# A hybrid decoder layer: down weights in 8 KB rows, other regions split, and some work ahead

## The chip, the core and the metric

The kernel runs on one core of a Trainium2 chip. The metric is the device time of one execution in microseconds. Engines are named as the profile names them: PE (matmul), PEld (weight load of PE), DVE (vector), ACT (scalar), POOL (GpSimd) and SP, whose queue issues nearly all the large loads. "Clock" is the TensorE clock that the throttle granted, as a share of full speed (1.0 is 2.4 GHz, 0.5 is 1.2 GHz).

## What is computed

One layer over 256 tokens of width 1024, in float32. What fills most of the time is the mixture of experts: 4 groups of 8 experts; every token goes to the best group and to two experts in it. The kernel streams the weights of all 32 experts (6 MB each) from memory.

```python
h = h + concat(pool_mixer(z), fox_attention(z)) @ w_out     # z = rms_norm(h) @ w_in
t = rms_norm(h)                                             # 256 x 1024
for g in range(4):                                          # top-1 group, top-2 experts in it
    hg = einsum('nd,edf->nef', t, w_e_gate[g])              # 8 x 1024 x 512
    hu = einsum('nd,edf->nef', t, w_e_up[g])                # 8 x 1024 x 512
    a  = silu(hg) * hu * comb[:, g, :, None]
    y  = y + einsum('nef,efd->nd', a, w_e_down[g])          # 8 x 512 x 1024
h = h + y
h = h + sigmoid(rms_norm(h) @ w_ple_gate) * (p @ w_ple_proj)
out = rms_norm(h)
```

## The kernel before

**Stages.** The first 105 us are the mixer (input projection, pooling, attention, output projection) and the start of the routing. Then tokens are sorted into slots by one-hot matrices: each expert has 32 slots, four experts (a quad) fill 128. `count` counts the tokens ahead of each, `first_slots` and `first_gather` make the one-hots of the first quad and gather its tokens, transposed, into `xg`. Experts then run as 16 pairs `pi` of experts 2pi and 2pi+1; pairs 2q and 2q+1 are quad `q`, quads 2g and 2g+1 are group `g`. Last stands the pair 15, which is written out by hand.

**A pair.** `gate_up(pi, 0)` and `gate_up(pi, 1)` multiply the gathered tokens by gate and up weights (rows k 0 to 3 and 4 to 7 of the 8 that lie in each partition, "kh0" and "kh1"); `hidden` applies SiLU; `hidden_transposes` turns the hidden activations; `down` multiplies by the down weights; `stack` evicts. `fill(pi, 0..3)` stands between these and runs small work planned for that place (`plan(pair, fill 0, fill 1, fill 2, fill 3)`): the gather of the next quad (`gather`, L910), its scatter weights (`scatter_weights`: DVE makes `oc`, L919, PE transposes it into `sw`, L922), the scatter of a finished quad (L982), and for a finished group the gate of the embedding: `turn` transposes its rows (L1097, evicted by DVE into `fin`, L1098), `z_direct` multiplies them by the gate weights `wpg` (L1108), `finish` writes the group's rows out. The order of instructions on PE, DVE and ACT is the written one (a manual schedule).

**The stream.** `load_pair(pi)` issues the twelve 1 MB loads of a pair on SP's queue (gate, up, then down), one pair ahead of their users. They go into 20 regions of 1 MB in SBUF (128 partitions of 8 KB), which `queue` hands out in turn; a region is free for its next load when the last reader of its old content is done. Three of the regions are pairs of half-regions, ("8a","8b"), ("9a","9b") and ("5a","5b"); a load into such a pair is two loads of 0.5 MB (`stream`, L798), a load into a whole region one (L801). Seven entries leave the ring: `xrows` (rows of a group), `PP` (embedding projections), `r_ht` (the turned rows `fin`) and four of gate weights `wpg`, so that 13 MB remain. Eight loads can be under way; the ninth issue waits until the eighth before it has landed.

**Rows.** Gate and up weights are laid out `(p k) f`: in a whole region a partition takes 4 rows of 512 floats that lie side by side in memory, 8 KB. Down weights are `(c p) d`: a partition takes two rows of 1024 floats that lie apart, 4 KB each. A load into half a region has rows of 4 KB too.

**The quarters.** Beside the regions lie four 4 KB-wide buffers Q0 to Q3 (`quarter`) in which `xg`, `ys`, attention tiles and others take turns.

Of the kernel before, what the change touches and what calls it, by code (L numbers as in the profile page):

```python
# [25 lines left out]
def layer_kernel(ctx, tc, x, p, g_mix, w_in, b_f, w_pool, s_pool, w_out, g_ffn, w_grp, b_grp,  # L26
# [575 lines left out]
    def half_logits(tb, dh):  # L602
        if dh == 0:
            psls[tb] = acc(f"ps_l{tb}")
        for k in range(4):
            nc.tensor.matmul(psls[tb][:, 0:36], lhsT=tTs[tb][:, dh, k, :], rhs=wr[:, dh, k, :],
                             start=dh == 0 and k == 0, stop=dh == 1 and k == 3)
# [90 lines left out]
    square_half(1, 1)  # L698
    half_transposes(1, 1)
    count(0)  # L700
    half_logits(1, 0)
# [85 lines left out]
    wd_v = w_e_down[0].rearrange("g e (c p) d -> (g e) p c d", p=128)  # L787
# [16 lines left out]
    def whole_region():  # L804
        return queue.pop(next(n for n, i in enumerate(queue) if not isinstance(i, tuple)))
# [9 lines left out]
    def load_last():  # L815

        gu, dn, used = {}, {}, []
        for j in range(2):
# [5 lines left out]
            for h in range(2):  # L824
                part = wd_v[e, :, :, 512 * h:512 * h + 512] if j else wd_v[e, :, 2 * h:2 * h + 2, :]
                dn[j, h] = stream(f"wd{e}{h}", part)[1]
# [3 lines left out]
    def load_pair(pi):  # L830
# [26 lines left out]
    Xc, auxc, rowi, smalls = {}, {}, {}, {}  # L857
# [13 lines left out]
    def compact(g):  # L871
# [7 lines left out]
        Xc[g] = xrows[:, (g % 2) * 1024:(g % 2 + 1) * 1024]  # L879
# [24 lines left out]
    def gather(q, kh, orr):  # L904
# [3 lines left out]
        pg = tb_(f"pgx{q}{kh}")  # L908
# [6 lines left out]
    def scatter_weights(q, oq):  # L915

        oc = wk.tile([128, 128], F32, tag="c2", name=f"oc{q}")
        e = 3 + 4 * (q % 2)
        nc.vector.tensor_tensor(oc.rearrange("p (e s) -> p e s", e=4), oq.rearrange("p (e s) -> p e s", e=4),  # L919
                                auxc[q // 2][:, e:e + 4, None].to_broadcast([128, 4, 32]), op=ALU.mult)  # L920
        pw = tb_(f"sw{q}p")
        nc.tensor.transpose(pw[:, 0:128], oc, ident)  # L922
# [70 lines left out]
    def embedding(p_in, wpp):  # L993
        psp = tb_("ps_p")
        for k in range(2):
            for tb in range(2):
                nc.tensor.transpose(psp[:, k * 256 + tb * 128:k * 256 + (tb + 1) * 128],
                                    p_in[:, tb, k * 128:(k + 1) * 128], ident)
        pT = wk.tile([128, 2, T], F32, tag="a", bufs=3, name="pT")
        nc.vector.tensor_copy(pT, psp.rearrange("p (k t) -> p k t", k=2))  # L1000
        for i in range(4):
# [4 lines left out]
            nc.scalar.copy(PP[:, i // 2, (i % 2) * 512:(i % 2 + 1) * 512], ps)  # L1006
# [25 lines left out]
    yss = {0: quarter(1, "ys0")}  # L1032
# [4 lines left out]
    xrows = region(whole_region(), "xrows")  # L1037
    compact(0)
    oq, orr = one_hots(0)
    scatter_weights(0, oq)  # L1040
    oq, orr = one_hots(1)
    stack(1, pd, yss[0])
    for kh in range(2):
        gather(1, kh, orr)
    scatter_weights(1, oq)
# [41 lines left out]
    def fin_tile(g):  # L1087

        return (big.tile([128, 2048], F32, tag="X", name=f"fin{g}") if g == LG else region(r_ht, f"fin{g}"))
# [3 lines left out]
    def turn(g, mh):  # L1093
        hT = fins[g][:, 0:1024].rearrange("p (m t) -> p m t", m=8)
# [66 lines left out]
    def dense_path():  # L1161
        tD = region(r_ht, "tD").rearrange("p (k t) -> p k t", k=8)
        for tb in range(2):
            for kh in range(2):
# [3 lines left out]
                nc.vector.tensor_copy(tD[:, 4 * kh:4 * kh + 4, tb * 128:(tb + 1) * 128],  # L1168
# [8 lines left out]
        for k in range(8):  # L1177
            nc.vector.scalar_tensor_tensor(tD[:, k, :], tD[:, k, :], gf[:, k:k + 1], rbd,
# [384 lines left out]
```

## Time and profile before

| | |
|---|---|
| median of 3 runs | 594.89 us (594.45 to 595.76) |
| the profiled execution | 595.37 us |
| its span (first to last instruction) | 593.8 us |
| mean granted clock | 0.929 |
| PE busy, share of the span | 89% |
| DVE, ACT, POOL busy | 29%, 20%, 7% |
| bytes read from memory | 220.93 MB |

The profiled execution is 0.48 us over the median of the runs, and 1.6 us of it lie around the span.

### The profile page before, as it was taken

The page shows a single profiled execution, that of the slowest core. Times are in us where ns is not written, and L with a number is a line of the kernel's source. Part 1 is how long each engine was busy: PE and PEld are TensorE (multiplying, and loading weights), DVE is VectorE, ACT ScalarE, POOL GpSimd, SP SyncE. Part 2 cuts the span into 40 slices and gives each one's busy share as a digit, 9 for nine tenths or more (in the row PEclk, how much of TensorE's full clock was granted, in tenths as well). Part 3 has the DMA queues.
Part 4 walks back from the last instruction along what each step waited for, and adds up shares of the span by engine and source line. Part 5 has one row for each costly group of instructions (what it writes and reads, how often), then busy time and mean ns, then how long its engine had stood idle before and what let it go on. Part 6 is the DMA issues. An engine that isn't in the chain of part 4 may idle for free.

```text
span 593.8 us, 7947 instructions
## 1 busy us (share of the span) xinstructions
PE 527.2 (89%) x3201; PEld 258.7 (44%) x3201; DVE 174.1 (29%) x453; ACT 116.2 (20%) x245; POOL 40.6 (7%) x83
## 2 busy tenths in 40 slices
PE   8999999888879997898789589989989889999991
PEld 7889778632423442232224143324343343334450
DVE  5768765422211122000141112042111120125124
ACT  4544553300101002000121001031101010102123
POOL 6087000000000000000000000000000000000100
PEclk9999999798889897899888799999998979999996
DMA  8989966599999999999999999999999999999920
GB/s 284 345 289 414 389 259 247 216 390 418 408 416 412 423 409 421 419 416 419 413 421 413 419 408 421 410 418 412 417 411 416 413 415 412 417 412 415 412 107 17
DMA packets 55734, 222.54 MB, mean 375 GB/s; under 512 B 8714, under 2 KB 15630, under 8 KB 42254
## 3 DMA queue, kind: packets, MB, share of 16 engines
q1 hardware_dynamic: 55086, 220.94, 93.3%
q0 software_dynamic: 608, 1.05, 0.5%
q8 instruction: 26, 0.43, 0.3%
q14 instruction: 14, 0.11, 0.0%
HBM read 220.93 MB, written 2.10 MB: 376 GB/s over the span
## 4 chain that ended last, share of the span: by engine, by line
PE 47%; DMA 38%; issue 6%; DVE 4%; ACT 2%; SPq 1%; POOLq 0%; POOL 0%; DVEq 0%; ACTq 0%
DMA wu<-in_w_e_up_dram 23%; PE pg L936 11%; DMA wd<-in_w_e_down_dram 9%; PE pd L964 5%; PE po L277 4%; PE Z L1108 3%; PE zl L1270 3%; DMA wpg<-in_w_ple_gate_dram 3%; PE pgx L910 2%; DMA wg<-in_w_e_gate_dram 2%; PE ps_k L277 2%; PE ps_q L277 1%; PE g L663 1%; PE pp L1004 1%; PE xc L884 1%
## 5 line engine op out<-in xcount | busy, mean ns | idle before, releaser
L936 PE MATMUL pg<-wu,xg 128*32 128x512 f32 x480 | 129.1, 639 | 13.8 <-DMA wu<-in_w_e_up_dram 13.8
L936 PE MATMUL pg<-wg,xg 128*32 128x512 f32 x472 | 122.3, 640 | 7.4 <-PEq L1393 5.2
L964 PE MATMUL pd<-wd,at 128*32 128x512 f32 x480 | 69.7, 710 | 3.1 <-issue 1.5
L1108 PE MATMUL Z<-wpg,fin 128*128 128x512 f32 x128 | 59.5, 606 | 2.1 <-DVE fin L1098 2.1
L943 DVE TENSOR_TENSOR act<-act,pg 64x512 f32<-64x512 f32 x15 | 10.4, 692 | 168.9 <-ACT act L942 168.9
L936 PEld LDWEIGHTS pg<-wg,xg 128*32 128x32 f32 x472 | 27.0, 116 | 63.1 <-issue 52.7
L936 PEld LDWEIGHTS pg<-wu,xg 128*32 128x32 f32 x480 | 30.8, 116 | 48.9 <-DMA wu<-in_w_e_up_dram 27.4
L942 ACT ACTIVATE act<-pg 64x512 f32<-64x512 f32 x15 | 8.8, 588 | 177.9 <-PE pg L936 177.9
L964 PEld LDWEIGHTS pd<-wd,at 128*32 128x32 f32 x480 | 16.8, 127 | 48.7 <-issue 44.6
L1108 PEld LDWEIGHTS Z<-wpg,fin 128*128 128x128 f32 x128 | 22.9, 189 | 34.5 <-issue 31.7
L972 DVE COPY ys<-pd 64x512 f32<-64x512 f32 x15 | 10.4, 694 | 85.5 <-ACT ys L971 78.8
L910 PE MATMUL pgx<-oq,xrows 128*128 128x128 f32 x112 | 30.6, 427 | 2.9 <-DVE xg L912 2.4
L1157 POOL DMA_INDIRECT out_dram<-fin,rowi x3 | 3.0, 1003 | 424.3 <-DVE ing L868 281.8
L910 PEld LDWEIGHTS pgx<-oq,xrows 128*128 128x128 f32 x112 | 27.6, 332 | 9.3 <-issue 4.2
L971 ACT COPY ys<-pd 64x512 f32<-64x512 f32 x15 | 8.6, 577 | 78.5 <-PE pd L964 78.5
L1270 PE MATMUL zl<-wpg,yT 128*64 128x512 f32 x96 | 23.2, 605 | 0.0
L277 PE MATMUL po<-sp_o,cTh 128*128 128x512 f32 x64 | 20.8, 405 | 0.0
L1131 PE MATMUL ppc<-PP,ing 128*128 128x512 f32 x32 | 14.8, 601 | 2.0 <-DVE ing L868 1.7
L912 DVE TENSOR_TENSOR xg<-pgx,gf 128x512 f32<-128x512 f32 x14 | 9.7, 692 | 18.6 <-PE pgx L910 18.6
L884 PE MATMUL xc<-X,ing 128*128 128x512 f32 x32 | 14.7, 602 | 0.0
L982 PE MATMUL Y<-ys,sw 128*128 128x512 f32 x28 | 13.9, 618 | 0.7 <-ACTq L1393 0.7
L277 PE MATMUL ps_k<-aTh,sp_k 128*128 128x256 f32 x64 | 12.6, 290 | 0.0
(361 smaller groups left out, 683.8 us busy)
## 6 DMA issues: line engine op xcount, KB each, us to landing
wu<-in_w_e_up_dram SPq DMA_DIRECT2D x52, 1024.0 KB, 16.3
wg<-in_w_e_gate_dram SPq DMA_DIRECT2D x49, 1024.0 KB, 16.8
wd<-in_w_e_down_dram SPq DMA_DIRECT2D x49, 1024.0 KB, 17.7
wd<-in_w_e_down_dram SPq DMA_DIRECT2D x30, 512.0 KB, 15.0
wg<-in_w_e_gate_dram SPq DMA_DIRECT2D x28, 512.0 KB, 15.2
wu<-in_w_e_up_dram SPq DMA_DIRECT2D x24, 512.0 KB, 15.2
w_o<-in_w_out_dram SPq DMA_DIRECT2D x4, 1024.0 KB, 5.7
wpg<-in_w_ple_gate_dram SPq DMA_DIRECT2D x4, 1024.0 KB, 15.7
```

The lines of the kernel that those rows point to most:

```text
L277: nc.tensor.matmul(o, lhsT=a, rhs=b, start=first and i == 0, stop=last and i == 2)
L884: nc.tensor.matmul(px, lhsT=pg_[:, tb, :], rhs=X[:, tb, ds], start=tb == 0, stop=tb == 1)
L910: nc.tensor.matmul(pg[:, k4 * 128:(k4 + 1) * 128], lhsT=Xc[q // 2][:, 4 * kh + k4::8], rhs=orr, start=True, stop=True)
L912: nc.vector.tensor_tensor(xgs[q][:, 4 * kh:4 * kh + 4, :], pg.rearrange("p (k t) -> p k t", k=4), gf[:, 4 * kh:4 * kh + 4, None].to_broadc ...
L936: nc.tensor.matmul(pg[32 * c:32 * c + 32, :], lhsT=xg[:, k, sl:sl + 32], rhs=gu["gu"[c // 2], j, kh](k % 4), start=k == 0, stop=k == 7, ti ...
L943: nc.vector.tensor_mul(act[64:128, :], act[64:128, :], pg[64:128, :])
L964: nc.tensor.matmul(pd[32 * gI:32 * gI + 32, :], lhsT=at[:, c, 32 * j:32 * j + 32], rhs=dn[j, c // 2](c % 2)[:, dh * 512:(dh + 1) * 512], s ...
L972: nc.vector.tensor_copy(ys[rs, 512:1024], pd[64:128, :])
L982: nc.tensor.matmul(Ys[g][dh], lhsT=sws[q], rhs=ys[:, dh * 512:(dh + 1) * 512], start=q % 2 == 0, stop=q % 2 == 1 or last)
L1108: nc.tensor.matmul(Z[g][i], lhsT=hTs[g][:, m, :], rhs=wpg[m // 2](m % 2)[:, 512 * i:512 * i + 512], start=m == 0, stop=m == 7)
L1131: nc.tensor.matmul(pp, lhsT=ings[g][:, tb, :], rhs=PP[:, tb, ds], start=tb == 0, stop=tb == 1)
L1270: nc.tensor.matmul(zls[pi][64 * dh:64 * dh + 64, :], lhsT=yTs[pi][:, m, :], rhs=wpg[m // 2](m % 2)[:, dh * 512:(dh + 1) * 512], start=m == ...
```

## The change

Down weights are laid out `(f p c) d`: of each half `f` of the 512 hidden rows, a partition takes two rows that lie side by side in memory, 8 KB. The hidden index of partition p is then 256 f + 2 p + c, so `hidden_transposes` picks every second column. `wpp` (the embedding projection's weights) is laid out in the same way. `xrows`, `PP` and `r_ht` take the three pairs of half-regions out of the ring; before they took the whole regions 15, 0 and 12.

Half a load more goes out early: of the first down weights of expert 3, which wait for region 8a (and 9a) until the first pair's `gate_up` has read it, one half is loaded into the quarter Q1 (`wd_extra`), and `ys0`, which lay there, lies in Q3.

Work is written in another order at several places: `count(1)` ahead of the last two of the first gather; three of the logits of tokens 128 to 255 ahead of the transposes before them; `oc` (`spread_weights`, DVE) is made in fill 0, and the transpose `sw` stands ahead of both halves of the gather, whose second half goes to another PSUM bank; `turn` stands in fill 2 (ahead of `down`) and not in fill 3 in pairs 4, 8 and 12; `finish(2)` stands in fill 0 of pair 14; one of four `z_scatter` of the last pair stands ahead of `down1(1, 0)`.

```diff
     square_half(1, 1)
+    half_logits(1, 0, range(3))
     half_transposes(1, 1)
     count(0)
-    half_logits(1, 0)
+    half_logits(1, 0, (3,))
     half_logits(1, 1)
 ...
-    first_gather(0, range(6))
+    first_gather(0, range(4))
     choose_group(1)
     choose_experts(1)
     count(1)
+    first_gather(0, (4, 5))
 ...
-    wd_v = w_e_down[0].rearrange("g e (c p) d -> (g e) p c d", p=128)
+    wd_v = w_e_down[0].rearrange("g e (f p c) d -> (g e) p f c d", f=2, c=2)
 ...
-    def whole_region():
-        return queue.pop(next(n for n, i in enumerate(queue) if not isinstance(i, tuple)))
+    def two_halves(i, name):
+        return [big.tile([128, 1024], F32, tag=f"R{z}", name=f"{name}{n}") for n, z in enumerate(i)]
+    def split_region():
+        return queue.pop(next(n for n, i in enumerate(queue) if isinstance(i, tuple)))
 ...
-                i, dn[j, ch] = stream(f"wd{e}{ch}", wd_v[e, :, 2 * ch:2 * ch + 2, :])
+                if (e, ch) == (3, 0):
+                    extra = quarter(1, "wd_extra")
+                    nc.sync.dma_start(extra, wd_v[e, :, 0, 0, :])
+                    i = queue.pop(0)
+                    rest = big.tile([128, 1024], F32, tag=f"R{i[0]}", name="wd_rest")
+                    nc.sync.dma_start(rest, wd_v[e, :, 0, 1, :])
+                    dn[j, ch] = lambda r: rest if r else extra
+                else:
+                    i, dn[j, ch] = stream(f"wd{e}{ch}", wd_v[e, :, ch])
                 used.append(i)
 ...
+            f0 = 256 * (c // 2)
-            nc.tensor.transpose(pa[:, c * 64:(c + 1) * 64], act[64:128, c * 128:(c + 1) * 128],
+            nc.tensor.transpose(pa[:, c * 64:(c + 1) * 64], act[64:128, f0 + c % 2:f0 + 256:2],
                                 ident[64:128, 64:128])
 ...
-        i, wpp = stream("wpp", w_ple_proj[0].rearrange("(k p) c -> p k c", p=128))
+        i, wpp = stream("wpp", w_ple_proj[0].rearrange("(p k) c -> p k c", k=2))
 ...
-    yss = {0: quarter(1, "ys0")}
+    yss = {0: quarter(3, "ys0")}
 ...
-    xrows = region(whole_region(), "xrows")
+    xrows = two_halves(split_region(), "xrows")
 ...
     def new_quad(q):
         oqs[q] = one_hots(q)
+        spread_weights(q, oqs[q][0])
 ...
-        return ([lambda: gather(q, 0, oqs[q][1])], [lambda: gather(q, 1, oqs[q][1]),
-                                                    lambda: scatter_weights(q, oqs[q][0])])
+        return ([lambda: scatter_weights(q), lambda: gather(q, 0, oqs[q][1])],
+                [lambda: gather(q, 1, oqs[q][1], acc)])
 ...
-            plan(at, [], [], [], [lambda e=e: e < LG - 1 and new_fin(e), lambda e=e: turn(e, 0), lambda e=e: turn(e, 1),
-                                 lambda e=e: half_norm(e)])
+            plan(at, [], [], [lambda e=e: e < LG - 1 and new_fin(e), lambda e=e: turn(e, 0), lambda e=e: turn(e, 1)],
+                 [lambda e=e: half_norm(e)])
 ...
-            plan(at + 2, [], [], end[1:])
+            plan(at + 2, end[1:])
 ...
-            PP = region(whole_region(), "PP").rearrange("p (b d) -> p b d", b=2)
+            PP = two_halves(split_region(), "PP")
 ...
-            r_ht = whole_region()
+            r_ht = split_region()
 ...
     hidden_transposes1(1)
+    z_scatter(Q, range(2, 3), 96)
     down1(1, 0, dn[1, 0])
-    z_scatter(Q, range(2, 4), 96)
+    z_scatter(Q, range(3, 4), 96)
```

Of each wide buffer's two halves the code now takes `PP[tb]`, `fins[g][0]`, `fins[g][1]` and `xrows[g % 2]` where it took slices; the down weights of the last expert are cut into four loads of 0.5 MB, each of rows of 2 KB as before (two loads before).

Three places in the order of instructions show what moved. The first is SP's queue at the start of pair 3's loads, where `wg` and `wu` are gate and up weights and the shape's last numbers are the rows of floats in each partition. Before:

```order
L801 DMA wpp<-in_w_ple_proj_dram 128x2x1024
L801 DMA wg_1647<-in_w_e_gate_dram 128x2048
L798 DMA wg_1649<-in_w_e_gate_dram 128x1024
L798 DMA wg_1650<-in_w_e_gate_dram 128x1024
L798 DMA wu_1653<-in_w_e_up_dram 128x1024
L798 DMA wu_1654<-in_w_e_up_dram 128x1024
L798 DMA wu_1657<-in_w_e_up_dram 128x1024
L798 DMA wu_1658<-in_w_e_up_dram 128x1024
L801 DMA wg_1661<-in_w_e_gate_dram 128x2048
```

The same place with the change:

```order
L804 DMA wpp<-in_w_ple_proj_dram 128x2048
L804 DMA wg_1649<-in_w_e_gate_dram 128x2048
L804 DMA wg_1651<-in_w_e_gate_dram 128x2048
L804 DMA wu_1653<-in_w_e_up_dram 128x2048
L801 DMA wu_1655<-in_w_e_up_dram 128x1024
L801 DMA wu_1656<-in_w_e_up_dram 128x1024
L804 DMA wg_1659<-in_w_e_gate_dram 128x2048
```

Two of three split loads have become whole ones of 8 KB rows; behind this piece one down load is split, and none else but the last expert's.

The second is PE in pair 12, from the end of `gate_up` (`pg`) to the first rows of `down` (`pd`); `pgx` is the gather, `pa` the hidden transposes, `ht` the turned rows. Before:

```order
L936 MATMUL pg_3371<-wu_3226,xg_3279 32x512
L910 MATMUL pgx_3416<-oq_3390,xrows 128x128 x4
L949 MATMUL pa_3422<-ident,act_3412 128x64 x4
L910 MATMUL pgx_3429<-oq_3390,xrows 128x128 x4
L922 MATMUL sw7p<-ident,oc_3435 128x128
L964 MATMUL pd_3441<-wd_3228,at_3427 32x512
L964 MATMUL pd_3441<-wd_3230,at_3427 32x512
```

The same place with the change:

```order
L960 MATMUL pg_3322<-wu_3183,xg_3242 32x512
L946 MATMUL sw7p<-ident,oc_3344 128x128
L931 MATMUL pgx_3373<-oq_3341,xrows_1578 128x128 x4
L974 MATMUL pa_3379<-ident,act_3365 128x64 x4
L931 MATMUL pgx_3386<-oq_3341,xrows_1578 128x128 x4
L1127 MATMUL ht_3392<-ident,xrows_1577 128x128 x4
L1127 MATMUL ht_3398<-ident,xrows_1577 128x128 x4
L989 MATMUL pd_3404<-wd_3185,at_3384 32x512
```

The transpose `sw7p` has gone ahead of both gathers, and the turned rows have come in from behind the sixteen rows of `pd`.

The third is PE in the first routing; `g` is a gather of the first quad by the one-hot `or`, `ps_cs` the count. Before:

```order
L663 MATMUL g_1274<-or_1148,X 128x128
L663 MATMUL g_1276<-or_1148,X 128x128
L638 LDWEIGHTS triu_bf
L638 MATMUL ps_cs_1286<-oh,triu_bf 128x32
L638 LDWEIGHTS triu_bf
L638 MATMUL ps_cs_1286<-oh,triu_bf 128x32
L638 LDWEIGHTS ones_bf
L638 MATMUL ps_cs_1286<-oh,ones_bf 128x32
```

The same place with the change:

```order
L638 LDWEIGHTS triu_bf
L638 MATMUL ps_cs_1282<-oh,triu_bf 128x32
L638 LDWEIGHTS triu_bf
L638 MATMUL ps_cs_1282<-oh,triu_bf 128x32
L638 LDWEIGHTS ones_bf
L638 MATMUL ps_cs_1282<-oh,ones_bf 128x32
L638 LDWEIGHTS ones_bf
L638 MATMUL ps_cs_1282<-oh,ones_bf 128x32
L663 MATMUL g_1287<-or_1148,X 128x128
L663 MATMUL g_1289<-or_1148,X 128x128
```

The count has gone ahead of the last two gathers.

## Rows read from the trace of the kernel before

**Rows 1.** Windows: stretch, length; PE, PEld, DVE, ACT, POOL busy (count); clock; DMA share; GB/s.

```profile
120.00:468.00 348.00, 303.35 (x1570) 115.82 (x1562) 65.99 (x175) 39.77 (x79) 2.04 (x2) 0.91 1.02 415
482.00:563.00 81.00, 79.40 (x557) 30.91 (x553) 19.07 (x43) 10.37 (x23) 3.32 (x9) 1.00 1.02 414
```

**Rows 2.** Waits of PE, 230 to 470 us: waiter, waited for, total us, times, longest.

```profile
PE pg L936 <- DMA wu<-in_w_e_up_dram: 13.8, 11, 1.7
```

**Rows 3.** Timeline of PE, where its last wait for a load ends.

```profile
468.42 0.62 PE L936 MATMUL pg<-wu,xg 128*32 128x512 f32 x1 [1.47 <-DMA wu<-in_w_e_up_dram]
```

**Rows 4.** Waits of PE, 468 us to the end.

```profile
PE sw7p L922 <- DVE oc L919: 1.1, 1, 1.1
PE Z L1108 <- DVE fin L1098: 1.0, 1, 1.0
...
PE pd L1449 <- issue: 0.4, 1, 0.4
PE yt L1260 <- ACT ys L971: 0.4, 1, 0.4
PE pgx L910 <- DVE xg L912: 0.4, 1, 0.4
```

**Rows 5.** Expert 31's last gate load, 549.3 us: issue, time to landing; its first user.

```profile
L801 SPq DMA_DIRECT2D wg<-in_w_e_gate_dram x1: 328/328/328, 549.3 to 549.3; - x1
...
DMA to landing us min/median/max: 13.9/13.9/13.9
...
566.74 0.12 PEld L1427 LDWEIGHTS pg<-wg,xg 128*32 128x32 f32 x2
```

**Rows 6.** Windows of 8 us within the stream.

```profile
212.00:220.00 8.00, 8.00 (x55) 3.03 (x46) 1.84 (x3) 0.59 (x1) 0.00 (x0) 1.00 1.03 410
364.00:372.00 8.00, 8.00 (x43) 2.65 (x41) 0.93 (x6) 0.00 (x0) 0.00 (x0) 1.00 1.01 420
226.00:234.00 8.00, 6.97 (x42) 2.53 (x35) 2.26 (x6) 1.81 (x5) 0.00 (x0) 0.80 1.02 420
```

**Rows 7.** DMA packets in 212 to 220 us, then 364 to 372.

```profile
DMA packets 877, 3.28 MB, mean 410 GB/s; under 512 B 77, under 2 KB 77, under 8 KB 877
...
DMA packets 462, 3.36 MB, mean 420 GB/s; under 512 B 52, under 2 KB 52, under 8 KB 52
```

**Rows 8.** DMA packets in 120 to 468 us, then 468 to 572.

```profile
DMA packets 28486, 144.25 MB, mean 415 GB/s; under 512 B 2854, under 2 KB 3110, under 8 KB 18738
...
DMA packets 9380, 41.29 MB, mean 397 GB/s; under 512 B 857, under 2 KB 857, under 8 KB 7323
```

**Rows 9.** Windows around the first `gate_up`.

```profile
113.00:119.00 6.00, 5.89 (x42) 2.43 (x45) 0.88 (x4) 2.87 (x9) 0.79 (x1) 0.70 0.09 26
114.40:116.60 2.20, 2.19 (x12) 0.67 (x16) 0.01 (x1) 2.18 (x7) 0.00 (x0) 0.50 0.00 0
```

**Rows 10.** Timeline of SP: issues of the first pairs' down weights.

```profile
117.46 1.28 SPq L798 DMA_DIRECT2D wd<-in_w_e_down_dram  x2
...
119.26 0.33 SPq L798 DMA_DIRECT2D wd<-in_w_e_down_dram  x1
```

**Rows 11.** Timeline of DVE and PE in the first routing.

```profile
111.35 0.29 DVE L648 TENSOR_TENSOR oq<-ps_cs,slot 128x128 f32<-128x128 f32 x1 [0.52 <-PE ps_cs L638]
...
112.02 2.28 PE L663 MATMUL g<-or,X 128*128 128x128 f32 x8 [0.71 <-DVE or L651]
```

**Rows 12.** Groups by line, PE: busy us, mean ns of one, idle before.

```profile
L949 PE MATMUL pa<-ident,act 64*128 64x64 f32 x60 | 6.9, 235 | 2.5 <-DVE act L943 1.5 <-DVE fin L1098 1.0
...
L1260 PE MATMUL yt<-ident,ys 64*128 64x64 f32 x24 | 3.7, 288 | 0.5 <-ACT ys L971 0.4
```

**Rows 13.** Timeline of PE: `down` of pair 12, and of pair 14.

```profile
478.64 5.21 PE L964 MATMUL pd<-wd,at 128*32 128x512 f32 x32
...
538.60 3.64 PE L964 MATMUL pd<-wd,at 128*32 128x512 f32 x32
```

**Rows 14.** Waits of SP, 120 to 460 us.

```profile
SPq L801 <- PE pa L949: 7.4, 2, 7.1
```

More of the change, by code (lines that the diff above doesn't have):

```diff
@@ L600, in half_transposes, with half_logits @@
         nc.scalar.copy(tTs[tb][:, dh], pt.rearrange("p (k t) -> p k t", k=4))
-    def half_logits(tb, dh):
-        if dh == 0:
+    def half_logits(tb, dh, ks=range(4)):
+        if tb not in psls:
             psls[tb] = acc(f"ps_l{tb}")
-        for k in range(4):
+        for k in ks:
             nc.tensor.matmul(psls[tb][:, 0:36], lhsT=tTs[tb][:, dh, k, :], rhs=wr[:, dh, k, :],
@@ L824, in load_last @@
             for h in range(2):
-                part = wd_v[e, :, :, 512 * h:512 * h + 512] if j else wd_v[e, :, 2 * h:2 * h + 2, :]
-                dn[j, h] = stream(f"wd{e}{h}", part)[1]
+                if j:
+                    w = region(queue.pop(0), f"wd{e}{h}").rearrange("p (f c d) -> p f c d", f=2, c=2)
+                    for f in range(2):
+                        nc.sync.dma_start(w[:, f], wd_v[e, :, f, :, 512 * h:512 * h + 512])
+                    dn[j, h] = lambda c, w=w: w[:, c // 2, c % 2, :]
+                else:
+                    dn[j, h] = stream(f"wd{e}{h}", wd_v[e, :, h])[1]
         queue.extend(used)
@@ L902, in one_hots, with gather @@
         return oo[:, 0, :], oo[:, 1, :]
-    def gather(q, kh, orr):
+    def gather(q, kh, orr, bank=tb_):
         if q not in xgs:
             xgs[q] = quarter((0, 2)[q % 2], f"xg{q}").rearrange("p (k s) -> p k s", k=8)
-        pg = tb_(f"pgx{q}{kh}")
+        pg = bank(f"pgx{q}{kh}")
         for k4 in range(4):
@@ L913, in gather, with spread_weights @@
                                 gf[:, 4 * kh:4 * kh + 4, None].to_broadcast([128, 4, 128]), op=ALU.mult)
-    def scatter_weights(q, oq):
-        oc = wk.tile([128, 128], F32, tag="c2", name=f"oc{q}")
+    def spread_weights(q, oq):
+        oc = ocs[q] = wk.tile([128, 128], F32, tag="c2", name=f"oc{q}")
         e = 3 + 4 * (q % 2)
@@ L1044, in layer_kernel @@
         gather(1, kh, orr)
-    scatter_weights(1, oq)
+    scatter_weights(1)
     gpm = gp.rearrange("p q k -> p (q k)")
@@ L1087, in fin_tile @@
     def fin_tile(g):
-        return (big.tile([128, 2048], F32, tag="X", name=f"fin{g}") if g == LG else region(r_ht, f"fin{g}"))
+        if g < LG:
+            return two_halves(r_ht, f"fin{g}")
+        t = big.tile([128, 2048], F32, tag="X", name=f"fin{g}")
+        return [t[:, 0:1024], t[:, 1024:2048]]
     fins = {}
     def turn(g, mh):
-        hT = fins[g][:, 0:1024].rearrange("p (m t) -> p m t", m=8)
+        hT = fins[g][0].rearrange("p (m t) -> p m t", m=8)
         pt = tb_(f"ht{g}{mh}")
@@ L1119, in z_again @@
         for i in range(4):
-            nc.tensor.matmul(Z[LG][i][:, 0:256], lhsT=ident, rhs=fins[LG][:, 256 * i:256 * i + 256], start=True,
+            nc.tensor.matmul(Z[LG][i][:, 0:256], lhsT=ident, rhs=fins[LG][0][:, 256 * i:256 * i + 256], start=True,
                              stop=False)
@@ L1130, in embedding_rows @@
         for tb in range(2):
-            nc.tensor.matmul(pp, lhsT=ings[g][:, tb, :], rhs=PP[:, tb, ds], start=tb == 0, stop=tb == 1)
+            nc.tensor.matmul(pp, lhsT=ings[g][:, tb, :], rhs=PP[tb][:, ds], start=tb == 0, stop=tb == 1)
         nc.scalar.activation(PPc[g][:, ds], pp, AF.Copy, scale=0.5)
@@ L1161, in dense_path @@
     def dense_path():
-        tD = region(r_ht, "tD").rearrange("p (k t) -> p k t", k=8)
+        tD = [t.rearrange("p (k t) -> p k t", k=4) for t in two_halves(r_ht, "tD")]
         for tb in range(2):
@@ L1208, in dense_path @@
                     nc.vector.scalar_tensor_tensor(xs, pdd[tb], cc[:, tb:tb + 1], xs, op0=ALU.mult, op1=ALU.add)
-        hD = region(r_ht, "hD").rearrange("p (m t) -> p m t", m=8)
+        hD = [t.rearrange("p (m t) -> p m t", m=4) for t in two_halves(r_ht, "hD")]
         for tb in range(2):
@@ L1303, in last_rows_home @@
         nonlocal last_o
-        last = region(r_ht, "last")
-        zs[NQ - 1], last_o = last[:, 0:1024], last[:, 1024:2048]
+        zs[NQ - 1], last_o = two_halves(r_ht, "last")
     def new_fin(g):
@@ L1348, in layer_kernel @@
         if g:
-            plan(at, [], [], [], [lambda e=e: e < LG - 1 and new_fin(e), lambda e=e: turn(e, 0), lambda e=e: turn(e, 1),
-                                 lambda e=e: half_norm(e)])
-            end = [lambda e=e: gates(e), lambda e=e: finish(e, fins[e][:, 1024:2048])]
+            plan(at, [], [], [lambda e=e: e < LG - 1 and new_fin(e), lambda e=e: turn(e, 0), lambda e=e: turn(e, 1)],
+                 [lambda e=e: half_norm(e)])
+            end = [lambda e=e: gates(e), lambda e=e: finish(e, fins[e][1])]
         if g == 1:
```

42 lines of the change are left out of this document (24 added, 18 removed).

## The prediction

> **What bounds the kernel now.** I read the table first (PE is busy for 89% of the span, so two bounds are possible, PE and the loads), and then windows. Between 120 and 468 us the DMA engines are busy all the time at 415 GB/s, while PE is busy for 303 of 348 us [rows 1]. The waits of PE say the same: eleven times the up weights of a pair are the last to come, 13.8 us in all [rows 2]. So up to 468 us the stream of weights sets the time. The last such wait ends at 468.42 us [rows 3]. From there to 563 us both are full: PE is busy for 79.4 of 81 us, and the stream still runs at 414 GB/s [rows 1]. PE's own idle places in that part are short and name no DMA: the gather waits for the DVE eviction of the last one (0.4), `sw7p` for `oc` (1.1), the gate product Z for `fin` (1.0), `yt` for `ys` (0.4), and `pd` of the last pair for nothing that the trace names (0.4) [rows 4]. The stream is close behind PE all the same: the last gate load for the last expert's second `gate_up` is issued at 549.3 and lands 13.9 us later, at 563.2; the up load beside it lands some 2.5 us after that, about 565.7 (my estimate: one more MB at 414 GB/s), and the user starts at 566.74 [rows 5]. The slack is about 1.1 us. So two sums are needed, one of the stream and one of PE after its last wait, and the smaller gain counts.
>
> **The change, part by part.** *Rows of 8 KB.* Two kinds of stretch occur in the stream. In 212 to 220 us all packets are under 8 KB, and the rate is 410 GB/s; in 364 to 372 all but 52 small ones are of 8 KB, and it is 420 [rows 6, 7]. I take 409.5 and 419.5 as the rates. The change turns nearly every two 4 KB packets of the stream into one of 8 KB: those of the down weights by their layout, those of gate and up weights because the ring holds no split region any more. Between 120 and 468 us there are 18738 packets under 8 KB, of which 3110 are under 2 KB and stay; of the other 15628 some 900 stay (seven loads of half a MB with 128 packets each). 14700 x 4096 bytes = 60.3 MB take 147.2 us at the one rate and 143.7 at the other: 3.5 us. Behind 468 us there are 7323 - 857 = 6466, less 1024 rows of 2 KB in the last expert's down weights: 5442 packets, 22.3 MB, 1.3 us [rows 8]. Bounds: nothing, if the rate goes by something other than row length; and about 1.9 times as much if the share of DMA time counts too (1.03 at 410 GB/s against 1.01 at 420, 2% on top of 2.4%, so 4.5% in all [rows 6]): 6.6 and 2.4 us. I take the middle, since the rates of pure stretches are just what is to be exchanged, and since the gate weights `wpg`, which have the form that all loads now get (8 KB rows, whole regions), ran at 420 GB/s in 226 to 234 us [rows 6].
>
> On such rows the Trainium skill, "DMA: Bandwidth & Descriptors", section "Why small descriptors are slow (HBM only)", puts a fixed cost of a few cycles on each packet beside its bytes; by its figures two packets of 4 KB cost about 1.1% more than one of 8 KB (an estimate), where the rows show 2.4%. By that the first two terms would be about 1.6 and 0.6 us. The direction is the same, the size less than half; the measured rates decide.
>
> *Half a MB of room.* Before, SP stands at expert 3's first down weights, which wait for regions 8a and 9a, and issues them at 117.46, when the first `gate_up` has read these [rows 10]; between 113 and 119 us the DMA engines are nearly idle (26 GB/s) [rows 9]. Now one half goes to Q1, which the output projection leaves ahead of that stretch, so 0.52 MB run in the gap: 0.52 / 0.41 = 1.28 us of stream. But at 117.46 one half load is released where there were two, and the next issue comes at 119.26 [rows 10], so up to half a microsecond may be lost to an empty queue. I take 0.9; bounds 0.6 and 1.3.
>
> *Count ahead of two gathers.* DVE's `oq` waits 0.52 us for the count, and the second quarter of the gather waits for `or` behind it [rows 11]. Two gathers (0.57 of the 2.28 us for eight) now stand behind the count: DVE is done up to 0.5 us sooner, PE has the same work. I take 0.2 us on the first `gate_up`, and so on the first releases of the ring; the lower bound is nothing. That `gate_up` ran at half clock (0.50 in 114.4 to 116.6) [rows 9]; if PE, with one pause less, kept full speed there, it would end 1.1 us sooner, and with 0.6 for the gathers at most 3.0 us would come out of the start. Start: 0.9 + 0.2 = 1.1 us. The logits that go ahead of transposes lie in PE's waits for the norm and cost nothing.
>
> *PE's order.* `oc` is made in fill 0, so `sw` no longer waits for it (1.07); the second gather has another bank and need not wait for the eviction (0.39); the turned rows are ready when `down` is done, so Z does not wait (1.03); `finish(2)` goes to pair 14's fill 0, out of the way of `ys` (0.42); and one `z_scatter` fills the 0.43 in front of `pd` [rows 4]. Ahead of 468 us such waits are worth nothing, since PE waits for the stream behind them. Behind it the first four are worth 2.9 us of PE's time; the fifth lies behind the last load's user and counts whichever bound holds. Against them: the hidden transposes read every second column. `yt`, of the same shape, does so already and takes 288 ns where `pa` takes 235 [rows 12]; twelve of them behind 468 us cost up to 0.6 us. I take half of it, since the two stand in stretches of different clock. The same work for DVE (`oc`, 0.3 us) moves into a stretch where it is idle four fifths of the time [rows 1].
>
> *Sums.* The stream to its end: 1.1 + 3.5 + 1.3 = 5.9, and the 1.1 us of slack that PE has to give: 7.0. PE: 1.1 + 3.5 until its last wait, then 2.9 - 0.3: 7.2. The stream's is the smaller; with 0.43 behind it the gain is 7.4 us. The profiled execution, 595.37, would become 588.0; the median of the runs lies 0.48 lower, so 594.89 - 7.4 = **587.5 us**. Pair 12's `down` ran at half clock for most of its time, 5.21 us where pair 14's took 3.64 [rows 13]; as the waits shift, such a stretch may come or go, 1.6 us each way.
>
> **The rivals.** *A, the forecast:* 585.5 to 589, chance 0.57. *A half:* only half of the rate difference is row length, the rest the number of loads or the regions. The terms are 1.75 and 0.65: 1.1 + 1.75 + 0.65 + 1.1 + 0.43 = 5.0, so 589.9 us. For it: no stretch changes row length alone. Chance 0.10. *B, row length does not set the rate:* 410 and 420 come from the regions written, or from what PE reads at the time. Then only the start, the slack and the last term remain: 1.1 + 1.1 + 0.43 = 2.6, 592.3 us; with the lower bounds, 0.6 and no slack, 593.9. Against it: `wpg` at 420 amid the same work. Chance 0.13. The Trainium skill, "DMA: Bandwidth & Descriptors", section "Specifications", has elements of 512 bytes suffice for the full rate, which would be this case; the two stretches speak against it, if nothing else differs between them. *C, more:* packet time shrinks by 4.5%, or the first `gate_up` gets full clock. The stream then goes out of PE's way, and PE's chain holds: 1.1 + 6.6 + 2.6 + 0.4 = 10.7, 584.2 us. Chance 0.12. *D, slower, the ring starves:* before, the ring's 13 MB were 16 loads (10 whole, 6 halves), so eight in flight held 6.5 MB; now they hold 8, and SP stands 1.5 MB, 3.7 us, nearer to what PE has still to release. SP already waits for `pa` twice, 7.1 us at the longest [rows 14]. Each such wait grows by up to 3.7 us, but starts to cost only where it exceeds the 8 MB in flight, 20 us of stream; one of 29 us would cost 9, more than the whole gain: 596.5 us. The longest would now be about 11. Chance 0.08, with every other way of getting slower in it. That the change does not do what it says is excluded for the loads by SP's rows.
>
> **How the numbers follow.** About 0.2%, 1.2 us, is what a measurement of this kernel can tell from no change. Faster by more: A, A half, C and B at its middle (0.05), together 0.84; within: the rest of B, 0.08; slower 0.08. The range goes from the far half of C to B's middle and leaves out D, the rest of B and C's end, 0.2: 583.5 to 592.5.
>
> **What the changed profile would show.** Right: packets of 2 to 8 KB in the stream fall from some 22,000 to some 2,000, and windows in mid-stream read 418 to 421 GB/s; the gap at 113 to 119 us carries half a MB more; PE has no idle time ahead of `sw` and Z behind its last wait for a load, and that ends at about 464 us; the stream ends some 6 us earlier. If the rate stays at 415 with those packets gone, B holds. If SP's waits for PE grow beyond 15 us and the rate falls in mid-stream, D does. What would make the forecast wrong with the rate as said: that PE holds the end after all, through a stretch at half clock first of all.

## The result, and the profile after

The changed kernel took 588.72 us (median of 4 runs, 588.15 to 589.13) against 595.33 for the kernel before on the same chips (4 runs, 594.45 to 596.22): ratio 0.9877, 95% interval 0.9859 to 0.9894. Timed once more it took 589.99 against 595.74: 0.9895 (0.9875 to 0.9914). The profiled execution took 588.78 us with a span of 587.2, at a mean clock of 0.955 (before 595.37, 593.8, 0.929).

The page of the changed kernel, rate in 40 slices, and its packets:

```profile
GB/s 286 342 293 416 361 287 246 274 336 423 417 419 420 421 420 417 422 422 420 421 421 422 418 421 422 421 420 418 425 420 421 420 422 420 420 420 421 416 111 18
DMA packets 44726, 222.53 MB, mean 379 GB/s; under 512 B 8202, under 2 KB 15118, under 8 KB 20750
```

The rate in mid-stream is flat at 417 to 425 GB/s, and of packets between 2 and 8 KB 5632 are left in the whole span. Windows of the changed kernel (stretch, length, busy times of PE, PEld, DVE, ACT, POOL, clock, DMA share, GB/s), the first around the first `gate_up`, the others before and behind PE's last wait for pair 12:

```profile
113.00:119.00 6.00, 5.89 (x48) 3.15 (x51) 0.89 (x4) 2.87 (x9) 0.00 (x0) 0.86 0.64 242
120.00:462.00 342.00, 299.52 (x1566) 118.28 (x1558) 66.57 (x176) 39.54 (x79) 2.83 (x3) 0.95 1.01 419
466.00:560.00 94.00, 92.55 (x660) 38.83 (x659) 21.56 (x47) 11.34 (x25) 3.31 (x9) 1.00 1.01 418
```

They answer to [rows 1] and [rows 9]: 419 GB/s where there were 415, 242 in the gap where there were 26, and no half clock behind pair 12. The waits of PE from 462 us to the end (waiter, waited for, total us, times, longest), and the wait in pair 14's `down` on the timeline:

```profile
PE pg L960 <- DMA wu<-in_w_e_up_dram: 1.4, 1, 1.4
PE pd L989 <- DMA wd<-in_w_e_down_dram: 1.3, 1, 1.3
PE Ze L1563 <- ACT zw L1559: 0.5, 1, 0.5
```

```profile
534.57 0.64 PE L989 MATMUL pd<-wd,at 128*32 128x512 f32 x4 [1.33 <-DMA wd<-in_w_e_down_dram]
```

The five waits of [rows 4] are gone. A new one has come: PE waits for the second half of pair 14's down weights. So the stream, not PE, set the end in this execution. PE's weight loads (PEld), which this view leaves out, wait longer at the same place:

```profile
534.56 0.16 PEld L989 LDWEIGHTS pd<-wd,at 128*32 128x32 f32 x8 [2.24 <-DMA wd<-in_w_e_down_dram]
```

To follow the stream apart from its start I count landed bytes of packets of 2 KB and more. The 34th MB had landed at 130.69 us before and 130.05 after, the 214th at 565.01 and 558.87: 0.64 us gained at the start, and 5.5 more over 180 MB.

### The profile page after: what moved, and what is told of

Read it like the earlier page. It is cut to its first block, busy times and chain, and to the rows that moved or that the text cites. A ratio compares the mean times of both kernels' runs of the same rounds, so it can differ in the third digit from the quotient of the medians.

```text
span 587.2 us, 7911 instructions
## 1 busy us (share of the span) xinstructions
PE 523.1 (89%) x3201; PEld 261.7 (45%) x3201; DVE 174.0 (30%) x453; ACT 116.2 (20%) x245; POOL 40.1 (7%) x83
## 4 chain that ended last, share of the span: by engine, by line
DMA 58%; PE 32%; issue 6%; DVE 2%; ACT 1%; SPq 0%; POOLq 0%; POOL 0%; DVEq 0%
DMA wu<-in_w_e_up_dram 40%; DMA wd<-in_w_e_down_dram 17%; PE pg L960 7%; PE po L277 4%; PE ps_u L277 2%; PE ps_k L277 2%; PE ps_q L277 2%; PE Z L1138 2%; PE pgx L931 1%; PE zl L1303 1%; DMA w_v<-in_w_in_dram 1%; PE g L663 1%; PE ps_v L277 1%; PE pd L989 1%; PE S L465 1%
## 5 line engine op out<-in xcount | busy, mean ns | idle before, releaser
L960 PE MATMUL pg<-wu,xg 128*32 128x512 f32 x480 | 131.9, 633 | 19.7 <-DMA wu<-in_w_e_up_dram 19.7
L989 PE MATMUL pd<-wd,at 128*32 128x512 f32 x472 | 60.0, 627 | 3.8 <-DMA wd<-in_w_e_down_dram 1.3
L277 PE MATMUL ps_u<-aTh,sp_u 128*128 128x256 f32 x64 | 13.5, 308 | 0.0
## 6 DMA issues: line engine op xcount, KB each, us to landing
wu<-in_w_e_up_dram SPq DMA_DIRECT2D x62, 1024.0 KB, 19.8
wg<-in_w_e_gate_dram SPq DMA_DIRECT2D x62, 1024.0 KB, 19.8
wd<-in_w_e_down_dram SPq DMA_DIRECT2D x58, 1024.0 KB, 19.8
```

The lines of the kernel that those rows point to most:

```text
L277: nc.tensor.matmul(o, lhsT=a, rhs=b, start=first and i == 0, stop=last and i == 2)
L960: nc.tensor.matmul(pg[32 * c:32 * c + 32, :], lhsT=xg[:, k, sl:sl + 32], rhs=gu["gu"[c // 2], j, kh](k % 4), start=k == 0, stop=k == 7, ti ...
L989: nc.tensor.matmul(pd[32 * gI:32 * gI + 32, :], lhsT=at[:, c, 32 * j:32 * j + 32], rhs=dn[j, c // 2](c % 2)[:, dh * 512:(dh + 1) * 512], s ...
```

## The experiments

Ratios are to the kernel before, timed in turn on the same chip. "Stream" is what the 34th to 214th MB gained, in the profiled execution.

| kernel | median, before, us | ratio (95%) | span | stream |
|---|---|---|---|---|
| changed | 588.72, 595.33 | 0.9877 (0.9859 to 0.9894) | 587.2 | 5.5 |
| e1 4 KB down rows | 591.80, 595.14 | 0.9940 (0.9922 to 0.9957) | 590.4 | 1.6 |
| e2 split regions in the ring | 590.73, 595.14 | 0.9925 (0.9906 to 0.9944) | 588.1 | 3.0 |
| e3 old order of PE | 593.20, 596.10 | 0.9940 (0.9917 to 0.9963) | 592.3 | 5.5 |
| e4 new order alone | 594.49, 596.10 | 0.9968 (0.9957 to 0.9978) | 594.7 | -0.1 |
| e5 no half load ahead | 589.59, 596.10 | 0.9883 (0.9863 to 0.9903) | 588.5 | 5.3 |
| e6 old count and logits | 590.75, 596.10 | 0.9911 (0.9894 to 0.9928) | 589.8 | 5.4 |
| e7 `finish(2)` in fill 2 | 587.86, 595.14 | 0.9873 (0.9855 to 0.9891) | 587.2 | 5.5 |
| e8 `finish(2)` cut in two | 588.23, 595.14 | 0.9878 (0.9857 to 0.9898) | 587.9 | 5.4 |
| e9 neither half load nor count | 590.40, 595.34 | 0.9918 (0.9896 to 0.9940) | 589.4 | 5.5 |
| e10 rows and regions alone | 593.02, 595.34 | 0.9955 (0.9939 to 0.9972) | 592.1 | 5.5 |
| changed, again | 589.99, 595.74 | 0.9895 (0.9875 to 0.9914) | 588.7 | 5.4 |
| e7, again | 589.80, 595.74 | 0.9888 (0.9866 to 0.9910) | 587.9 | 5.5 |

**Row length or number of loads (e1, e2).** Theory: row length sets the rate. Rival: the number of loads, or the half regions, do. Of e1's edit, then of e2's:

```diff
-    wd_v = w_e_down[0].rearrange("g e (f p c) d -> (g e) p f c d", f=2, c=2)
+    wd_v = w_e_down[0].rearrange("g e (c p) d -> (g e) p c d", p=128)
...
-act[64:128, f0 + c % 2:f0 + 256:2]
+act[64:128, c * 128:(c + 1) * 128]
...
```

```diff
...
-queue.pop(next(n for n, i in enumerate(queue) if isinstance(i, tuple)))
+queue.pop(next(n for n, i in enumerate(queue) if not isinstance(i, tuple)))
```

> The changed kernel with the down weights laid out (c p) d again: two rows of 4 KB per partition and MB, still one load per MB; all else as changed. About 60 MB of the stream go back to 4 KB packets, out of the 82 MB that the change took from them. Theory 'rows' (row length sets the rate, 410 against 420 GB/s): the stream loses 60/82 of the 5.5 us that it gained between its 34th and 214th MB, 4.0 us; rate in mid-stream 415 to 416 GB/s; 592.7 us. Rival 'loads' (the number of loads, or the half regions, set the rate): nothing is lost, rate 419 to 420, 588.7 us.

> The changed kernel with the three split regions in the ring again (xrows, PP and r_ht take whole ones); down weights keep their layout, rows of 8 KB in whole regions and of 4 KB in halves. Some 75 loads of half a MB, 39 MB, go back to 4 KB packets. Theory 'rows': 39/82 of 5.5 us lost, 2.6 us; rate 417 GB/s; 591.3 us. Rival 'loads': the whole 5.5 us are lost, rate 414 to 415; 594.2 us. Rival 'starving ring' (fewer MB in flight are better): no loss or a gain against the changed kernel.

The DMA view of 240 to 460 us, each from its own trace: the kernel before, the changed one, e1, e2.

```profile
DMA packets 18208, 91.38 MB, mean 415 GB/s; under 512 B 1879, under 2 KB 1879, under 8 KB 12246
```

```profile
DMA packets 12918, 92.58 MB, mean 421 GB/s; under 512 B 1561, under 2 KB 1561, under 8 KB 1690
```

```profile
DMA packets 16387, 91.75 MB, mean 417 GB/s; under 512 B 1546, under 2 KB 1546, under 8 KB 8846
```

```profile
DMA packets 15856, 91.96 MB, mean 418 GB/s; under 512 B 1887, under 2 KB 1887, under 8 KB 7392
```

The packets between 2 and 8 KB are 10367, 129, 7300 and 5505, or 42.5, 0.5, 29.9 and 22.5 MB. Against the changed kernel 1.20, 0.83 and 0.62 MB fewer have moved: 2.86, 2.82 and 2.82% of the 4 KB bytes beyond its own 0.5 MB. The loss is in proportion to these bytes, whether they come from whole loads with two rows (e1, which has no more split loads than the changed kernel) or from half loads (e2). By stream, e1 lost 3.9 us (4.0 expected), e2 2.5 (2.6 expected). The rival falls: e1 should have lost nothing by it. The times moved by about as much, 2.7 to 3.7 and 1.8 to 2.9 us by the ratios' difference to the two timings of the changed kernel; e1's transposes are cheaper (below).

**What PE's order is worth (e3, e4, e10).** e3 puts back the old places of `oc`, `sw`, second gather, `turn`, `finish(2)` and `z_scatter`; e4 is the kernel before with these new places alone; e10 is the kernel before with layout and regions alone. Of e3's edit:

```diff
-        spread_weights(q, oqs[q][0])
-        return ([lambda: scatter_weights(q), lambda: gather(q, 0, oqs[q][1])],
-                [lambda: gather(q, 1, oqs[q][1], acc)])
+        return ([lambda: gather(q, 0, oqs[q][1])], [lambda: gather(q, 1, oqs[q][1]),
+                lambda: spread_weights(q, oqs[q][0]), lambda: scatter_weights(q)])
-            plan(at, [], [], [lambda e=e: e < LG - 1 and new_fin(e), lambda e=e: turn(e, 0), lambda e=e: turn(e, 1)],
-                 [lambda e=e: half_norm(e)])
+            plan(at, [], [], [], [lambda e=e: e < LG - 1 and new_fin(e), lambda e=e: turn(e, 0), lambda e=e: turn(e, 1),
+                                 lambda e=e: half_norm(e)])
...
```

> The changed kernel with PE's order behind the first routing as before: oc, sw and the second gather, turn, finish(2) and z_scatter at their old places; stream, regions, wd_extra and count as changed. Theory 'PE's chain' (with the faster stream PE's own chain behind pair 12 sets the end, and the old waits 0.39, 1.07, 1.03, 0.42 and 0.43 are back in it): against the run with only finish(2) undone, where PE holds the end, 2.9 us more, 590.8 us; no wait for a load behind pair 12. Rival 'stream' (the stream sets the end and the order of PE hides in it): only 0.43 comes back and the early write goes, 588.3 us.

> The kernel before with PE's new order alone (sw, second gather, turn, finish(2), z_scatter); layout, regions, loads, count as before. Theory 'stream': the stream of before is at most 1.1 us behind PE, so no more than this slack and 0.43 come out, less what the earlier output write costs (1.1 us on pair 14's down weights): 593.6 to 594.7 us, and PE waits for loads in pair 14. Rival 'PE': the 2.9 us and 0.43 of PE's waits come out, 591.8 us.

> The kernel before with the rows of 8 KB and the split regions moved, nothing else: no half load ahead, count and PE's order as before. Theory 'both bounds': the stream gains 3.9 us up to pair 12's last load, and PE's chain behind it stays as it was, so the gain is 3.9 us and not the 5.5 that the stream gains to its end: ratio 0.9935. Rival 'stream alone': 5.5 us and more, ratio 0.991 or less. Rival 'PE alone': PE's pauses eat it, ratio over 0.997.

The waits of PE in e3 behind 466 us, and a window of it:

```profile
PE sw7p L946 <- DVE oc L940: 1.1, 1, 1.1
PE Z L1138 <- DVE fin L1128: 1.0, 1, 1.0
PE Ze L1561 <- ACT zw L1557: 0.5, 1, 0.5
PE pd L1480 <- issue: 0.4, 1, 0.4
PE yt L1292 <- ACT ys L996: 0.4, 1, 0.4
PE pgx L931 <- DVE xg L933: 0.2, 1, 0.2
```

```profile
473.50:480.30 6.80, 5.73 (x29) 1.96 (x32) 0.89 (x2) 0.27 (x1) 0.00 (x0) 0.50 1.01 419
```

All the waits are back, no load is among them but pair 12's, and so is a stretch at half clock in pair 12, where before had it too. e3's stream gained the same 5.5 us, yet the time gained 3.6 us instead of 6.3 to 7.3: theory "PE's chain" holds (its 590.8 against a before of 595.1 is a ratio of 0.9927, within the interval); the stretch at half clock was not in the sum. e10 shows the same bound, with a stream as fast and a gain of 2.7 us; I had expected 3.9, which lies just outside its interval. In its trace the last wait for a load ends 3.0 us earlier than before (465.40 against 468.42), and PE takes 1.3 us more from there: the strided transposes cost about 0.7 of it (under *PE's order*), and pair 12's `down`, at half clock in both, the other 0.7, 5.89 us where it was 5.21 [rows 13]. The `down` of pair 12 in e10, then in the changed kernel:

```profile
475.62 5.89 PE L987 MATMUL pd<-wd,at 128*32 128x512 f32 x32
```

```profile
472.94 3.64 PE L989 MATMUL pd<-wd,at 128*32 128x512 f32 x32
```

In e4 PE waits for loads instead:

```profile
PE pg L959 <- DMA wu<-in_w_e_up_dram: 3.7, 3, 1.5
PE pd L988 <- DMA wd<-in_w_e_down_dram: 1.5, 1, 1.5
PE Ze L1562 <- ACT zw L1558: 0.5, 1, 0.5
```

Its gain of 1.9 us is what the slack of PE allowed, as theory "stream" has it (593.4 on a before of 595.33, 593.6 at best by the expectation, within the interval). e9 (below) has both parts without the start and gains 4.9 us, about the sum of e4 and e10, 1.9 + 2.7; what is left to 6.3 to 7.3 is the start's.

**The early write (e7, e8).** POOL writes group 2's rows at 522.74 us in the changed kernel, while pair 14's last down weights are under way, and at 544.81 before. e7's edit:

```diff
-            plan(at + 2, end[1:])
+            plan(at + 2, [], [], end[1:])
```

e8 leaves the sums of `finish(2)` where the change put them (called with False it stops ahead of its last two products, which stand in `finish_rows`), and moves these and the write:

```diff
...
-            plan(at + 2, end[1:])
+            plan(at + 2, [lambda e=e: finish(e, fins[e][1], False)])
...
-         zr(13, 6, 7) + [lambda: gained(14), last_rows_home, lambda: z_scatter(NQ - 2, range(4))])
+         zr(13, 6, 7) + [lambda: gained(14), lambda: finish_rows(2, fins[2][1]), last_rows_home,
+                         lambda: z_scatter(NQ - 2, range(4))])
```

> The changed kernel with finish(2) back in fill 2 of pair 14. In the changed kernel PE waits 1.33 us for pair 14's last down weights, which land at 534.52; group 2's output rows (0.5 MB) are now written from 522.7 us on, ahead of them, where they were written from 544.8 on before. Theory 'write' (this half MB stands in the stream ahead of the down weights and costs them 1.1 us): PE's wait there falls to about 0.2 us, the wait of yt for ys (0.42) comes back; 588.0 us. Rival 'stream' (the loads come when they come, the write costs nothing): the wait stays at 1.3 us, and 0.4 is lost; 589.1 us.

> The changed kernel with finish(2) cut in two: its sums stay in fill 0 of pair 14, its last two multiplications and the write of the rows go to fill 3, behind the transposes of pair 14's rows. Theory 'write': pair 14's last down weights land about 1.1 us sooner, PE waits for them no more than 0.2 us, no wait for ys; the last expert's up weights (landed at 559.4, used at 560.57 in the changed kernel) are then used as they land; 587.6 us. Rival 'stream': 588.7 us, and the wait of 1.3 us stays.

> The changed kernel with finish(2) back in fill 2 of pair 14, beside the changed kernel itself. Theory 'write with a tie' (without the early write the loads of pair 14 come in time, but PE, busy without a pause from pair 12's last load, holds the end at nearly the same place): 0.3 to 0.9 us faster than the changed kernel, no wait for a load behind pair 12. Rival 'no worth': within 0.3 us of it.

> The changed kernel once more, on one chip with the next run. 588.7 us if the before of this chip is at 595.3; ratio 0.9877.

The waits of PE in e7 behind 465 us name neither the down weights nor `ys` any more:

```profile
PE pg L960 <- DMA wu<-in_w_e_up_dram: 1.4, 1, 1.4
PE Ze L1563 <- ACT zw L1559: 0.5, 1, 0.5
```

But its weight loads still wait, for pair 14's down weights and now also for pair 15's up weights:

```profile
534.06 0.16 PEld L989 LDWEIGHTS pd<-wd,at 128*32 128x32 f32 x8 [1.04 <-DMA wd<-in_w_e_down_dram]
545.06 0.11 PEld L1459 LDWEIGHTS pg<-wu,xg 128*32 128x32 f32 x2 [0.38 <-DMA wu<-in_w_e_up_dram]
```

The tile views of pair 14's last down load in e7, to be held against the changed kernel's 21.0 us (further down), and of the last expert's second up load, 19.8 us in the changed kernel:

```profile
DMA to landing us min/median/max: 19.8/19.8/19.8
```

```profile
DMA to landing us min/median/max: 21.1/21.1/21.1
```

With the late write the down weights land 1.2 us sooner after their issue (19.8 in both executions of e7, 20.3 in e8; 21.0 to 21.1 in the changed kernel's two, e5, e6 and e9). So the write does delay the down weights by what theory "write" had. But when it is late, the loads behind it are late in their turn: the last expert's up weights took 21.1 and 22.0 us in e7's two executions and 20.9 in e8, 19.8 and 19.9 in the changed kernel's two. So the time did not follow. In both first executions the last expert's second `gate_up` starts at 560.57, while its up weights landed at 559.41 in the changed kernel and at 560.12 in e7. "PE, busy without a pause", as the expectation of the second timing has it, is not what the traces show; loads still hold PE up in e7, and so e3's expectation, which took e7 for PE's bound, began from a time that loads set in part.

Beside each other on one chip e7 is at 0.9888 and the changed kernel at 0.9895. Their profiled executions there have streams that stand alike (214th MB at 558.79 and 558.70 us), and e7's span is 0.8 us shorter; the medians differ by 0.2 us. The version with a late write beats the kernel before, not measurably the changed one, and "write with a tie" and "no worth" cannot be told apart.

The write moves 0.26 MB and not the half MB that the expectations had; the DMA view of 521 to 531 us of the changed kernel:

```profile
q0 software_dynamic: 143, 0.26, 6.8%
```

At 418 GB/s that is 0.6 us of stream (an estimate). Why the loads behind it lose 1.2 stays open.

**The start (e5, e6, e9).** e5 takes back `wd_extra`, e6 the places of count and logits, e9 both.

```diff
-                if (e, ch) == (3, 0):
+                if (e, ch) == (3, 99):
-    yss = {0: quarter(3, "ys0")}
+    yss = {0: quarter(1, "ys0")}
```

```diff
-    half_logits(1, 0, range(3))
-    half_logits(1, 0, (3,))
+    half_logits(1, 0)
-    first_gather(0, range(4))
+    first_gather(0, range(6))
-    first_gather(0, (4, 5))
```

> The changed kernel without the half load ahead: expert 3's first down weights wait for 8a and 9a as before, ys0 is back in Q1. Theory 'half a MB': the stream stands 1.28 us (0.52 MB at 410 GB/s) less what two releases at once give back, so 0.6 to 1.3 us later at its 34th MB, counted from the end of the output projection, and the end moves with it: 589.3 to 590.0 us. Rival 'hidden': the gap is filled by what follows, no difference, 588.7 us.

> The changed kernel with count(1) behind all six gathers and the logits behind the transposes, as before. Theory 'small': the first gate_up starts 0.2 us later from the end of the output projection, nothing else, 588.9 us. Rival 'clock': the pause of PE ahead of the gathers is back, and with it the half clock through the whole of the first gate_up (before 0.50 in 114.4 to 116.6 us; with the change PE is at full clock there): 0.6 to 1.7 us later, 589.3 to 590.4 us.

> The changed kernel without both parts that move the start of the stream (the half load ahead, the count and the logits). Theory 'start': counted from the end of the output projection, the 36th MB of the stream lands 1.8 us later than in the changed kernel (30.6 against 28.8 us), and as the stream sets the time up to pair 12 and PE has no pause behind it, the end moves by that: ratio to before 0.9877 to 0.9895 plus 0.003, so 0.991 to 0.992. Rival 'lost on the way' (the ring catches up, PE's waits for releases take the start's gain): ratio within 0.001 of the changed kernel.

The mixer ahead took 104.7 to 106.9 us in these executions, so I count from the end of the output projection: the end of the first `gate_up`, and the landing of the stream's 36th MB.

| us from the end of the output projection | first `gate_up` ends | 36th MB lands |
|---|---|---|
| neither (before, e4, e9, e10) | 17.7 to 18.1 | 30.1 to 30.9 |
| half load only (e6) | 17.3 | 30.5 |
| count and logits only (e5) | 16.3 | 30.3 |
| both (changed, twice; e1, e2, e3, e7, twice; e8) | 16.1 to 17.5 | 28.3 to 30.0 |

Window 113 to 119 us of e6, then of the changed kernel's second execution, to be held against the 242 GB/s and the clock of 0.86 of its first:

```profile
113.00:119.00 6.00, 5.89 (x42) 2.56 (x45) 0.90 (x4) 2.87 (x9) 0.00 (x0) 0.73 0.39 150
```

```profile
113.00:119.00 6.00, 5.89 (x43) 1.98 (x46) 0.55 (x3) 2.65 (x9) 0.00 (x0) 0.74 0.42 156
```

So this window cannot tell e6 from the changed kernel. In the table, each part alone left the 36th MB where it was without them, and both moved it by 0.8 to 1.8 us (30.6 before, 28.8 and 29.8 in the changed kernel's two). But e5 and e6 are one execution each, and among those with both parts the clock makes a difference of the same size: where half clock reached into the first `gate_up` (changed, again; e7, again; e8) it ended at 17.3 to 17.5, where it did not or hardly did, at 16.1 to 16.4. That half a MB of room is worth nothing while the releases behind it come late is what e6's one execution suggests.

By time, e6 at 0.9911 is worse than the changed kernel's two timings by 1.0 to 2.0 us, e9 by 1.4 to 2.4. Both have the direction of theory "start", and e9 the size (0.991 to 0.992 expected); only against the first timing do the intervals not overlap (e6's just touches), so the size is not settled. Theory "clock" is not shown: e6 is at half clock until 116.2 us, but the changed kernel's second execution is so until 116.1. e5, at 0.9883, cannot be told from the changed kernel by time, so its theory "half a MB" is seen in the stream (36th MB 1.5 and 0.5 us later than in the changed kernel's two executions) and not at the end.

## Why the prediction was right, and where its terms were off

*The bound.* Right: the stream before pair 12, then two bounds, and the smaller of two gains at the end. e3 and e10 show PE's bound, e4 the stream's. PE's sum was too small (below): the changed kernel's PE stood still for pair 14's loads, so the stream held by more than the 0.2 us between 7.0 and 7.2.

*Rows.* Right, and the size close: 3.5 + 1.3 = 4.8 us forecast, 5.5 measured. The rate term was small by 0.7, since a byte in 4 KB rows cost 2.8% more than one in 8 KB rows, where the pure stretches gave 2.4. Rivals B and A half are refuted by e1 and e2. The Trainium skill's fixed cost per packet ("DMA: Bandwidth & Descriptors", "Why small descriptors are slow (HBM only)") points the right way, and by the same runs the estimate of 1.1% worked out from it is too little (2.8% measured).

*The start.* 1.1 us forecast, 0.64 measured in the profile. Counted from the output projection the gain was 1.8 (0.8 in the second execution), and the output projection ended 1.13 us later in that execution, with a stretch at half clock at 32.8 us that before's execution did not have; e2, e5 and e6 did not have it either, so it belongs to the execution. The working was off in its parts, as far as single executions show: 0.2 us for count and logits looks too small (e6: 1.0 to 2.0 us), and the 0.9 for the half MB did not come alone. What the prediction kept for rival C, a first `gate_up` at full clock that ends 1.1 + 0.6 us sooner, did come in the profiled execution (16.1 against 17.7 us from the output projection) and not in the second (17.3). The misses of start and rows go against each other, so it is partly luck that the stream's sum is so close: 5.9 forecast, 6.1 measured.

*The end.* The slack was put at the last expert's up weights; in the changed kernel it was used up at pair 14's down weights. These landed 4.8 us earlier than before (the tile views, issue and time to landing; before, then changed):

```profile
L801 SPq DMA_DIRECT2D wd<-in_w_e_down_dram x1: 368/368/368, 522.8 to 522.8; - x1
DMA to landing us min/median/max: 16.5/16.5/16.5
```

```profile
L804 SPq DMA_DIRECT2D wd<-in_w_e_down_dram x1: 327/327/327, 513.5 to 513.5; - x1
DMA to landing us min/median/max: 21.0/21.0/21.0
```

The stream itself had gained 5.8 us there (202nd MB); the earlier write of group 2's rows, which the forecast costed at nothing, took 1.0 us of it back (1.2 by e7's landing times). With the slack of 1.1 us before (landing at 539.3; use half way through the row of `down` that begins at 538.60, about 540.4 [rows 13]) and the waits of 0.42 and 0.43 behind that place, 4.8 + 1.1 + 0.85 = 6.75; the span fell by 6.6. Against the forecast of 7.4 the miss is 0.8 us: the write's 1.2, less the 0.42 of `ys` that was not in the stream's sum.

*PE's order.* Forecast 2.9 - 0.3 + 0.43 of PE's time. The waits went as said. The strided transposes cost more than the half of their bound that I took; groups by line, changed kernel and e1 (which reads adjacent columns again):

```profile
L974 PE MATMUL pa<-ident,act 64*128 64x64 f32 x60 | 10.3, 292 | 2.5 <-DVE act L967 1.5 <-DVE fin L1128 1.0
```

```profile
L974 PE MATMUL pa<-ident,act 64*128 64x64 f32 x60 | 6.9, 235 | 2.5 <-DVE act L967 1.5 <-DVE fin L1128 1.0
```

3.4 us over 15 pairs, 0.23 a pair, so 0.7 us in the three pairs from pair 12 on, over the 0.6 that was the bound, and some more in the last pair. It is hidden where PE waits for loads. The half clock in pair 12 went away in the changed kernel, and its `down` took 3.64 us instead of 5.21, the 1.6 us that the prediction named and left out of the sum. The stream did not let this gain through: PE's weight loads wait for pair 14's loads instead.

*Rival D.* The ring did not starve: the rate stayed flat with 8 MB under way, and SP's longest wait for PE in 120 to 460 us was 6.4 us, where it had been 7.1 [rows 14]:

```profile
SPq L804 <- PE pg L960: 17.0, 16, 6.4
```

## What to carry to other kernels

When a stream of weights sets the pace, count its packets by size: two layouts with equal bytes can differ by the length of their rows, here by 2.8% between rows of 4 and of 8 KB, and the loss was in proportion to the bytes in the shorter rows. Before removing an engine's waits, find which of two bounds lies just behind: here faster rows alone gained 2.7 us of the 5.5 that the stream gained, a better order alone 1.9, both 4.9, and with an earlier start 6.3 to 7.3. A write travels in the same stream as the loads: moved ahead or back, it delays those that come behind it, so see which of them has slack. Look at the waits of the weight loads as well as those of the matmuls before you say that an engine runs without a pause.

## What the runs showed that was not expected

The same loads land later, measured against the bytes that have moved, in some executions: the changed kernel's wait for pair 14's down weights ended at 534.57 us in one execution and at 536.06 in the other, though the 202nd MB had landed at 530.17 and 529.97. These weights were issued 1.5 us later and took 21.0 us in both, so the lag is older: a load of gate weights that is issued at 438.9 us in both took 19.7 us in the one and 21.4 in the other. That is 1.5 us at the end from neither rate nor order; its cause stays open.

Stretches at half clock fall in different places in executions with the same instructions up to there (at 32.8 us, at 10 to 12 us, or nowhere in the mixer), and those in the mixer go with an output projection that ends 0.3 to 2.2 us later. With 4 to 6 runs a difference of 0.2% between two of these kernels cannot be told.
